# Group A's score operands laid out in runs, its strided queries copied side by side, and negated scores in groups A and B

## The chip, the core and the metric

The kernel runs on one core of a Trainium2 chip. The metric is the device time of one execution in microseconds (us), the median of several runs. TensorE (PE) multiplies, VectorE (DVE), ScalarE (ACT) and GpSimd (POOL) work element by element, and SyncE (SP) issues the DMAs. Each engine takes its own instructions in a fixed order.

## What is computed

One layer of a decoder whose 16 heads fall into four groups of four, all on 2048 tokens of width 1024. Cut to what matters here:

```python
h = rms_norm(x, norm_w) @ w_in            # one projection for all groups
# A: three causal windows, merged by their softmax denominators
DILATED_CONFIGS = ((128, 1), (512, 4), (2048, 16))   # (window, rate r)
for window, rate in DILATED_CONFIGS:
    # tokens folded by residue of r; 128 + 1 keys back within a residue class
    o, lse = banded_attention(fold(q), fold(k), fold(v), table, window // rate, dist_scale=rate)
# B: window of 128 with a learned sink in the softmax
# C: differential attention; D: compressed, selected and window branches
y = concat(A, B, C, D) * silu(gate)
x = x + y @ w_out
```

In each attention a score is q.k plus a bias by distance; the row's maximum is taken off before the exponential.

## The kernel before

**Stages.** The projection runs group by group (C, D, A, B) as a filler behind the attention of C, then D. Its helper `turn` (L735) turns queries and keys to feature rows by PE transposes (L741), and stores them as a high and a low half in the DRAM tensors `TQ` and `TK`, token by token along the row. Then `group_ab` (L1616) computes A and B, with the output projection `out_proj` (L2065) as its filler, and what is left of it ends the program.

**Group A, strided.** `ORDER` lists 32 units: for each head first r=16 and then r=4, four units of four query tiles each. `qk_load` (L1577) brings a head's queries and keys into `QK[h % 2]`: heads 0 and 2 into one big tile, `wb`, for both; heads 1 and 3 into a tile `AQ` for the queries and `keys` for the keys. `a_unit` (L1628) then makes for each query tile two PE matmuls (L1646, the two halves of the keys) of 128 columns, or 256 with the tile before it. Queries (the operand that stays in the array) and keys (the one that streams) are read with a step of r:

```python
def cols(j, i0, n):
    rho, i = divmod(q0 + j, nb)
    c0 = rho + r * 128 * (i - i0)
    return slice(c0, c0 + (n - 1) * r + 1, r)
```

r=16 gives 128 matmuls of 128 columns; r=4 gives 32 of 128 and 96 of 256. One DVE instruction (L1651) adds the bias `H` to the scores out of PSUM, stores the sum and keeps the row's maximum; a second small one (L1656) negates two maxima into column 65 of `AO`; ACT (L1662) takes the exponential with this as bias. Then come transposes (L393), a split into halves (L399 on ACT, L403 on DVE), the products with the values (L422), and the turn back (L435, L439 or L442 and L444). When a head's r=4 units end, `merge` (L1748) joins them with the r=16 result on POOL (L1761 to L1764).

**A with r=1, and B.** After the strided units, 16 units of A with r=1 (`make_a1`, L1829) alternate with 16 of B (`make_b`, L1929). r=1 uses the same `a_unit` with contiguous queries and keys. B has its own scores (L1948), bias and maximum (L1953), maximum with the sink (L1958) and negation (L1959).

**Order.** Nothing is scheduled on the chip. A planner in the kernel, `drive` (L302), writes the order: it keeps a clock per engine, adds an assumed cost for each instruction (`op`), and takes the next ready step of up to three open units, or three matmuls of the output projection where nothing else is ready. POOL also has the gate product of the output projection (L2113) in this stretch.

Of the kernel before, what the change touches and what calls it, by code (L numbers as in the profile page):

```python
# [102 lines left out]
def tile_hybrid_heads(ctx, tc, a):  # L103
# [355 lines left out]
    expo = const.tile([128, 32], F32, name="expo")  # L459
# [8 lines left out]
    sink = const.tile([128, 4], F32, name="sink")  # L468
    nlam = const.tile([128, 1], F32, name="nlam")
# [22 lines left out]
    def raw(t):  # L492
        return t.bitcast(F32)
# [137 lines left out]
    def project(g, first=None):  # L631
# [104 lines left out]
        def turn(t3, j, gi, keep):  # L736
# [3 lines left out]
            for i in range(4):  # L740
                PE.transpose(ps[:, i * 128:(i + 1) * 128], keep[i][0][:, j * 128:(j + 1) * 128], ident)  # L741
# [834 lines left out]

    def qk_load(h, x):  # L1577

        q, k = QK[h % 2]
        n = S // 2  # L1580
        if x < 2:
            aready[h] = load_q(q[:, x * n:(x + 1) * n].unsqueeze(1), "A", h, 1, x * n, n)
        else:
            c = slice((x - 2) // 2 * n, ((x - 2) // 2 + 1) * n)
            aready[h] = mv(raw(k)[x % 2::2, :, c], TK["A"][h * 64:h * 64 + 64, :, c])

# [29 lines left out]
    def group_ab():  # L1616
      with tc.tile_pool(name="aw", bufs=2) as aw, tc.tile_pool(name="as", bufs=1) as as_:
# [8 lines left out]


        def a_unit(r, q0, setup, room, need, source, stats, close):  # L1628
# [5 lines left out]
            def scores(half):  # L1634
                qs, ks, H = source()
                if half == 0:
                    st["P"] = aw.tile([128, 4, 256], F32, name="ap", bufs=3)
                    st["mx"] = aw.tile([128, 4], F32, name="amx", bufs=4)
                P, mx, O = st["P"], st["mx"], stats()
                slot = take("s")  # L1640
                ps = ps_s.tile([128, 512], F32, name="s")
                for j in (2 * half, 2 * half + 1):
                    n = 128 * (1 + prevs[j])
                    s0 = (j % 2) * 256
                    for x in range(2):
                        PE.matmul(ps[:, s0:s0 + n], lhsT=qs(j), rhs=ks(x, j, prevs[j]), start=(x == 0), stop=(x == 1))  # L1646
                        e = op("PE", mm(n) if r == 1 else max(217.0, 0.92 * n)) + 60.0
                for j in (2 * half, 2 * half + 1):
                    n = 128 * (1 + prevs[j])
                    s0 = (j % 2) * 256  # L1650
                    V.tensor_tensor_reduce(P[:, j, :n], ps[:, s0:s0 + n], rev(H, n - 1, n), 1.0, LOW,  # L1651
                                           OP.add, OP.max, mx[:, j:j + 1])
                    e = op("DVE", vv(n), e)
                give(slot, e)
                two = slice(2 * half, 2 * half + 2)
                V.tensor_scalar(O[:, two, 65], mx[:, two], -1.0, None, op0=OP.mult)  # L1656
                e = op("DVE", 72.0, e)

                def weights():
                    for j in (2 * half, 2 * half + 1):  # L1660
                        n = 128 * (1 + prevs[j])
                        A.activation(P[:, j, :n], P[:, j, :n], AF.Exp, bias=O[:, j, 65:66], accum_out=O[:, j, 64:65])  # L1662
                        st["e"] = op("ACT", av(n, 2), e)
                    st["half"] = st.get("half", 0) + 1
                defer(e, weights)

# [22 lines left out]
        def make_a(n):  # L1689
# [8 lines left out]

            def setup():
                if h < 3 and 1 <= n % 8 <= 6:  # L1700
                    qk_load(h + 1, n % 8 - 1)
                if q0 == 0:
# [15 lines left out]
            def source():  # L1718
                Q, K = QK[h % 2]

                def cols(j, i0, n):
                    rho, i = divmod(q0 + j, nb)
                    c0 = rho + r * 128 * (i - i0)
                    return slice(c0, c0 + (n - 1) * r + 1, r)
                return (lambda j: Q[:, cols(j, 0, 128)]), (lambda x, j, p: K[:, x, cols(j, p, 128 * (1 + p))]), Hs[h, r]
# [57 lines left out]
            def room():  # L1783
                if not have_all("A"):
# [3 lines left out]
            u = a_unit(r, q0, setup, room, lambda: max(at("s"), aready[h]), source,  # L1788
                       lambda: tiles(res[h, r][0]), close)
# [39 lines left out]
        def make_a1(m):  # L1829
            q0, h = AORDER[m]  # L1830

            def source():
                Q, K, lo = As[m][0], As[m][1], As[m][7]
                return ((lambda j: Q[:, j * 128:(j + 1) * 128]),
                        (lambda x, j, p: K[:, x, (q0 + j - p - lo) * 128:(q0 + j + 1 - lo) * 128]), raw(A1H(h)))
# [12 lines left out]
            def setup():  # L1848
                if m == 0:
# [3 lines left out]
                    parts += [as_.tile([128, 1024], F32R, name="ow%d" % i) for i in range(2)]  # L1853
# [75 lines left out]
        def make_b(n):  # L1929
# [3 lines left out]
            def scores(i):  # L1933
                Kb, Vb, Qb, lo, _ = Bs[g, t0]
                if i == 0:
                    st["P"] = aw.tile([128, 4, 256], F32, name="ap", bufs=3).rearrange("p (i j) c -> p i j c", i=2)
                    for x in ("mx", "nm", "den"):
                        st[x] = as_.tile([128, 4], F32, name="b" + x, bufs=5)
                P, mx, nm, den = st["P"], st["mx"], st["nm"], st["den"]
# [11 lines left out]
                for j in range(2):  # L1951
                    s0 = j * 256
                    V.tensor_tensor_reduce(P[:, i, j, :n], ps[:, s0:s0 + n], rev(BH[2 * g + j], n - 1, n), 1.0, LOW,  # L1953
                                           OP.add, OP.max, mx[:, i * 2 + j:i * 2 + j + 1])
# [3 lines left out]
                V.tensor_tensor(nm[:, c], mx[:, c], sink[:, 2 * g:2 * g + 2], op=OP.max)  # L1958
                V.tensor_scalar(nm[:, c], nm[:, c], -1.0, None, op0=OP.mult)  # L1959
                e = op("DVE", 260.0, e)  # L1960

                def weights():
                    for j in range(2):
                        x = i * 2 + j
                        A.activation(P[:, i, j, :n], P[:, i, j, :n], AF.Exp, bias=nm[:, x:x + 1],
                                     accum_out=den[:, x:x + 1])
# [271 lines left out]
```

## Time and profile before

| | |
|---|---|
| median of 3 runs | 1769.04 us (1765.94 to 1773.90) |
| profiled execution | 1773.27 us, span 1771.5 us |
| PE busy | 97% of the span |
| DVE, ACT, POOL busy | 76%, 61%, 39% |
| granted TensorE clock, mean | 0.988 |

A line of the profile names the engine, the source line, what is written and read (buffer numbers left out), the shape, and how often. "Busy" of PE is a sum of pipelined matmuls whose durations overlap, so the spacing of matmuls is read from the chain of waits: pieces in order of time, each with its start, its length and the number of instructions in it. The stage of group A's strided units goes from about 1348.5 to 1493.5 us.

### The profile page before, as it was taken

The numbers are of one execution on the slowest core, as the hardware profiler recorded it, in microseconds if no ns is written. First come the engines' busy times: TensorE is split into PE (matmuls) and PEld (weight loads), VectorE is DVE, ScalarE is ACT, GpSimd is POOL, SyncE is SP. The second block draws the span as 40 slices with busy tenths as digits, with TensorE's granted clock in tenths as the row PEclk, the third lists the DMA queues.
The fourth block names the chain that finished last, engine by engine and source line by source line (L and its number), as shares of the span: only waits on it lengthen the run. The fifth ranks groups of instructions, "written<-read, shape, count | busy, mean of one in ns | idle before, by whom it ended". The sixth has DMA issues, their size and how long they took to land.

```text
span 1771.5 us, 31769 instructions
## 1 busy us (share of the span) xinstructions
PE 1709.5 (97%) x10035; PEld 1503.3 (85%) x10035; DVE 1338.3 (76%) x4072; ACT 1072.3 (61%) x2588; POOL 692.8 (39%) x841
## 2 busy tenths in 40 slices
PE   7999999999998999899999999999999999999999
PEld 5878878888887889788888889899979999789987
DVE  4446689898999998488747868888366876888873
ACT  4345466656776756467646656777356776576651
POOL 4567554544544554211255552222521112433331
PEclk9999999999999999899999999999999999999999
DMA  7763554444445424642367533232375778999986
GB/s 246 223 198 108 184 171 144 121 118 139 116 143 159 146 91 152 188 117 88 125 194 226 170 108 96 59 97 85 105 238 169 233 226 259 278 313 311 320 283 213
DMA packets 283480, 308.24 MB, mean 174 GB/s; under 512 B 80256, under 2 KB 201216, under 8 KB 282640
## 3 DMA queue, kind: packets, MB, share of 16 engines
q1 hardware_dynamic: 283312, 306.21, 55.8%
q8 instruction: 80, 1.31, 0.3%
q14 instruction: 88, 0.72, 0.1%
HBM read 219.47 MB, written 86.92 MB: 173 GB/s over the span
## 4 chain that ended last, share of the span: by engine, by line
PE 51%; DVE 3%; issue 1%; DMA 1%; ACT 1%; POOL 0%; SPq 0%; DVEq 0%; POOLq 0%
PE j L840 11%; PE j L2159 9%; PE o L422 9%; PE pt L393 8%; PE s L1646 4%; PE s L950 4%; PE pt L435 3%; PE s L1336 1%; PE pt L2123 1%; PE s L1948 1%; PE s L1435 1%; PE pt L741 0%; DVE pl L403 0%; PE j L1164 0%; DMA xt<-in_xt_dram 0%
## 5 line engine op out<-in xcount | busy, mean ns | idle before, releaser
L840 PE MATMUL j<-wb,xh 128*128 128x512 f32 (+2 forms) x2048 | 618.2, 382 | 18.8 <-DVE wb L622 9.6
L840 PEld LDWEIGHTS j<-wb,xh 128*128 128x128 f32 x2048 | 373.1, 190 | 67.4 <-DVE wb L622 14.5
L840 PE MATMUL j<-wb,xl 128*128 128x512 f32 (+2 forms) x1024 | 385.4, 376 | 0.6 <-POOL xl L577 0.6
L399 ACT ACTIVATE ph<-pt 128x512 fp32r<-128x512 f32 (+4 forms) x486 | 266.0, 575 | 123.5 <-PE pt L393 117.0
L403 DVE TENSOR_TENSOR pl<-pt,ph 128x512 fp32r<-128x512 f32 (+4 forms) x486 | 311.9, 658 | 38.1 <-ACT ph L399 37.2
L840 PEld LDWEIGHTS j<-wb,xl 128*128 128x128 f32 x1024 | 194.3, 190 | 25.7 <-POOL xl L577 1.2
L679 POOL TENSOR_TENSOR ss<-ss,expo 128x6 f32<-128x6 f32 (+2 forms) x64 | 117.4, 1835 | 169.2 <-DVE ss L677 155.3
L577 POOL TENSOR_TENSOR xl<-xt,xh 128x512 fp32r<-128x512 f32 x112 | 149.2, 1333 | 9.3
L371 ACT ACTIVATE ot<-o 128x512 f32<-128x512 f32 (+1 forms) x160 | 81.5, 509 | 106.4 <-PE o L422 105.9
L571 POOL TENSOR_SCALAR xh<-xt 128x512 fp32r<-128x512 f32 x128 | 84.6, 661 | 134.2 <-DMA xt<-in_xt_dram 65.5
L950 PE MATMUL s<-keys,Q 128*128 128x512 f32 (+3 forms) x320 | 113.6, 400 | 12.7 <-DVE mx L952 6.1
L2113 POOL TENSOR_TENSOR xt<-xt,sq 128x512 f32<-128x512 f32 x32 | 41.3, 1290 | 184.2 <-PE s L1646 66.2
L952 DVE CUSTOM_DVE_ANT_0 prow<-s,Hs 128x512 f32<-128x512 f32 (+3 forms) x160 | 95.1, 604 | 19.3 <-PE s L950 18.8
L1066 DVE SCALAR_TENSOR_TENSOR pa<-pb,ra,pa 128x1024 f32<-128x1024 f32 (+4 forms) x96 | 107.5, 1147 | 2.3
L660 ACT ACTIVATE stqk<-j 128x512 f32<-128x512 f32 x64 | 38.2, 597 | 113.5 <-PE j L840 111.0
L952 DVE CUSTOM_DVE_ANT_0 pa<-s,H 128x512 f32<-128x512 f32 (+3 forms) x160 | 93.8, 603 | 14.0 <-PE s L950 11.3
L952 DVE CUSTOM_DVE_ANT_0 pb<-s,H 128x512 f32<-128x512 f32 (+3 forms) x160 | 93.1, 603 | 7.2 <-PE s L950 6.5
L1662 ACT ACTIVATE ap<-ap,AO 128x128 f32<-128x128 f32 (+1 forms) x192 | 86.4, 456 | 17.7 <-DVE AO L1656 17.5
L1050 ACT ACTIVATE pa<-pa,nm 128x128 f32<-128x128 f32 (+7 forms) x64 | 76.9, 1202 | 31.5 <-DVE nm L958 31.0
L674 DVE TENSOR_REDUCE ss<-sq 128x6 f32<-128x384 f32 (+2 forms) x64 | 39.3, 614 | 69.9 <-ACT sq L664 69.9
L435 PE MATMUL pt<-ident,ot 128*128 128x128 f32 x512 | 85.0, 278 | 3.1 <-ACT ot L371 2.6
L1050 ACT ACTIVATE pb<-pb,nm 128x128 f32<-128x128 f32 (+7 forms) x64 | 76.8, 1200 | 16.5 <-DVE nm L958 16.3
(267 smaller groups left out, 4207.4 us busy)
## 6 DMA issues: line engine op xcount, KB each, us to landing
xt<-in_xt_dram SPq DMA_DIRECT2D x128, 256.0 KB, 3.3
xr<-in_x_dram SPq DMA_DIRECT2D x16, 512.0 KB, 5.4
Q<-tqC SPq DMA_DIRECT2D x64, 128.0 KB, 3.4
DQ<-tqD SPq DMA_DIRECT2D x16, 512.0 KB, 4.8
raw<-gate_d SPq DMA_DIRECT2D x32, 256.0 KB, 4.2
stqk<-in_x_dram SPq DMA_DIRECT2D x32, 256.0 KB, 4.8
acc_d<-stqk SPq DMA_DIRECT2D x32, 256.0 KB, 4.5
stqk<-acc_d SPq DMA_DIRECT2D x32, 256.0 KB, 4.5
```

The costliest lines, as they stand in the source:

```text
L393: PE.transpose(ps[:rows, x * 128:(x + 1) * 128], src(), ident)
L399: A.activation(ph[:rows, :n], ps[:rows, :n], AF.Copy)
L403: V.tensor_tensor(pl[:rows, :n], ps[:rows, :n], ph[:rows, :n], op=OP.subtract)
L422: PE.matmul(u["po"][:, c0:c0 + wd], lhsT=lhsT(), rhs=x[:rows, col:col + wd], start=u["k"] == 1, stop=u["k"] == total, skip_group_check=True)
L435: PE.transpose(ps[:, i * 128:(i + 1) * 128], ot[:, i * 128:(i + 1) * 128], ident)
L577: G.tensor_tensor(l, xt, h, op=OP.subtract)
L679: G.tensor_tensor(ss[:, :nh], ss[:, :nh], expo[:, :nh], op=OP.pow)
L840: PE.matmul(ps[:, :n], lhsT=xx[:, ks], rhs=W[k][ww][:, lo:hi], start=(k == 0 and i == 0), stop=(k == KT - 1 and i == 2))
L950: PE.matmul(ps[:, :n], lhsT=q(), rhs=k[:, k0:k0 + n], start=(i == 0), stop=(i == np_ - 1))
L952: V.tensor_tensor_reduce(st["row"][:, k0:k0 + n], ps[:, :n], rev(H, t * 128 + 127 - k0, n), 1.0, LOW, OP.add, OP.max, st["mx"][:, ci:ci + 1])
L1050: A.activation(row[:, :nk], row[:, :nk], AF.Exp, bias=nm, accum_out=den[:, i, m:m + 1])
L2159: PE.matmul(ps, lhsT=xx[:, ks], rhs=OW[half, (k, c)][ww], start=(x == 0 and k == 0 and i == 0), stop=(x == len(halves) - 1 and k == 3 and ...
```

## The change

Keys of A are stored in another order of columns: the transposes of `turn` write each tile of 128 tokens by residue of 16, so that 8 keys of one residue stand side by side. Scores then stream the keys in runs of 8: r=16 takes one run of each tile; r=4 takes four residues, tile by tile; r=1 takes 16 residues. For r=4 and r=1 the scores stand in PSUM in another order of keys than the bias, so the DVE instruction reads PSUM with a jump at each element. The queries of a strided unit are copied side by side by POOL (`gather_more`), into four half tiles of the two `ow` tiles that take output weights later. The r=16, r=4 and r=1 query gains, and B's, are multiplied by -0.125 in place of 0.125, and the bias vectors of A's and B's heads are negated; so the DVE instruction takes a minimum, which is at once the negated maximum, ACT gets a scale of -1, and L1656 and L1959 go.

```diff
-        V.tensor_scalar(gains[:, 1:4], gains[:, 1:4], 0.125, None, op0=OP.mult)
+
+        V.tensor_scalar(gains[:, 1:3], gains[:, 1:3], -0.125, None, op0=OP.mult)
+        V.tensor_scalar(gains[:, 3:4], gains[:, 3:4], 0.125, None, op0=OP.mult)
...
+        V.tensor_scalar(nsink, sink, -1.0, None, op0=OP.mult)
...
-        V.memset(tp[96:128, :], NEG)
+        V.memset(tp[96:128, 0:8], -NEG)
+        V.memset(tp[96:128, 8:16], NEG)
+        V.tensor_scalar(tb[0:96, 0:8], tb[0:96, 0:8], -1.0, None, op0=OP.mult)
...
-                PE.transpose(ps[:, i * 128:(i + 1) * 128], keep[i][0][:, j * 128:(j + 1) * 128], ident)
+                to = ps[:, i * 128:(i + 1) * 128]
+                if g == "A" and j >= 2:
+                    to = to.rearrange("p (r i) -> p i r", r=16)
+                PE.transpose(to, keep[i][0][:, j * 128:(j + 1) * 128], ident)
...
+        def gather_more():
+            while len(AC) < len(ORDER) and ORDER[len(AC)][0] in aloaded and free("AC", 4) < INF:
+                n = len(AC)
+                h, r, q0 = ORDER[n]
+                hd = alloc("AC", 4)
+                C = OW4[hd[1] % 4 // 2][:, hd[1] % 2 * 512:hd[1] % 2 * 512 + 512]
+                Q = QK[h % 2][0].rearrange("p (c r) -> p r c", r=r)
+                if r == 16:
+                    G.tensor_copy(C.rearrange("p (j c) -> p j c", j=4), Q[:, q0:q0 + 4])
+                else:
+                    G.tensor_copy(C, Q[:, q0 // 4])
+                AC[n] = (C, hd, op("POOL", 1150.0, max(aready[h], hd[2])))
...
-                        e = op("PE", mm(n) if r == 1 else max(217.0, 0.92 * n)) + 60.0
+                        e = op("PE", mm(n)) + 60.0
...
-                    V.tensor_tensor_reduce(P[:, j, :n], ps[:, s0:s0 + n], rev(H, n - 1, n), 1.0, LOW,
-                                           OP.add, OP.max, mx[:, j:j + 1])
+
+                    fr = ps[:, s0:s0 + n] if r == 16 else ps[:, s0:s0 + n].rearrange("p (b u) -> p u b", b=16 // r)
+                    V.tensor_tensor_reduce(P[:, j, :n], fr, rev(H, n - 1, n), 1.0, -LOW,
+                                           OP.add, OP.min, O[:, j, 65:66])
...
-                two = slice(2 * half, 2 * half + 2)
-                V.tensor_scalar(O[:, two, 65], mx[:, two], -1.0, None, op0=OP.mult)
-                e = op("DVE", 72.0, e)
...
-                return (lambda j: Q[:, cols(j, 0, 128)]), (lambda x, j, p: K[:, x, cols(j, p, 128 * (1 + p))]), Hs[h, r]
+                K, C = QK[h % 2][1], AC[n][0]
+                if r == 16:
+                    K = K.rearrange("p x (t r c) -> p x r t c", t=16, r=16)
+                    ks = lambda x, j, p: K[:, x, q0 + j]
+                else:
+                    K = K.rearrange("p x (t s a c) -> p x a s t c", s=4, a=4, c=8)[:, :, q0 // 4]
+                    ks = lambda x, j, p: K[:, x, :, (j - p) * 4:(j + 1) * 4]
+                return (lambda j: C[:, j * 128:(j + 1) * 128]), ks, Hs[h, r]
...
-                        (lambda x, j, p: K[:, x, (q0 + j - p - lo) * 128:(q0 + j + 1 - lo) * 128]), raw(A1H(h)))
+                        (lambda x, j, p: K[:, x].rearrange("p (t b c) -> p b t c", b=16, c=8)[:, :, q0 + j - p - lo:q0 + j + 1 - lo]),
+                        raw(A1H(h)))
...
-                V.tensor_tensor(nm[:, c], mx[:, c], sink[:, 2 * g:2 * g + 2], op=OP.max)
-                V.tensor_scalar(nm[:, c], nm[:, c], -1.0, None, op0=OP.mult)
-                e = op("DVE", 260.0, e)
+                V.tensor_tensor(nm[:, c], nm[:, c], nsink[:, 2 * g:2 * g + 2], op=OP.min)
+                e = op("DVE", 130.0, e)
```

The planner's assumed cost of a strided score falls with it (`mm(n)`), so the order of the whole stage is another one. A copy is written into the order when its head's last load has been issued and one of the four half tiles is free, and the scores of a unit wait for its copy.

On PE, the order at the start of the strided stage, before (`s` are scores, `j` the output projection, `pt` transposes, `wb` here the queries and keys of head 0):

```order
L1646 MATMUL s<-wb 128x128 x12
L2159 MATMUL j<-wb,xh 128x512 x2
L2159 MATMUL j<-wb,xl 128x512
L1646 MATMUL s<-wb 128x128 x4
L2123 MATMUL pt<-ident,xt 128x128 x4
L393 MATMUL pt<-ident,ap 128x128 x4
```

and now (`ow` are the copied queries, L1675 the scores, L2199 the output projection):

```order
L1675 MATMUL s<-wb,ow_17192 128x128 x8
L2199 MATMUL j<-wb,xh 128x512 x2
L2199 MATMUL j<-wb,xl 128x512
L1675 MATMUL s<-wb,ow_17192 128x128 x8
L2199 MATMUL j<-wb,xh 128x512 x2
L2199 MATMUL j<-wb,xl 128x512
L393 MATMUL pt<-ident,ap 128x128 x4
L1675 MATMUL s<-wb,ow_17193 128x128 x8
```

Three matmuls of the output projection now stand behind each unit of eight scores, where before one such three stood behind twelve scores. Over the strided stage their number goes from 90 to 144, and behind the last score from 237 to 180.

On POOL, the order from group D's last sum (L1553) over the first two merges (L1761 to L1764) before, with what each instruction waits for:

```order
L1553 TENSOR_TENSOR Os<-Os,yps 128x128 [waits DMAHW1_49,Pool_49]
L2113 TENSOR_TENSOR xt<-xt,sq 128x512 [waits DMAHW4_49,DMAHW5_49,DVE_49,PE_49] x2
L1761 TENSOR_TENSOR AO<-AO,mg 128x16x65 [waits DMAHW2_49,PE_49,DMAHW7_49,Activation_49,Pool_49]
L1761 TENSOR_TENSOR AO<-AO,mg 128x16x65 [waits DMAHW7_49,DMAHW2_49,DVE_49]
L1763 TENSOR_TENSOR AO<-AO 128x16x65 [waits Pool_49]
L1764 COPY AO<-mgn 128x16
L2113 TENSOR_TENSOR xt<-xt,sq 128x512 [waits DMAHW0_49,DMAHW1_49,DVE_49,PE_49]
```

and now, around the first merge (L1801 to L1804; L1651 and L1653 are the copies for r=16 and r=4, from `AQ` those of head 1, from `wb` those of head 2; L2153 is the gate product):

```order
L1653 COPY ow_17192<-AQ 128x512 [waits PE_49,Pool_49] x2
L2153 TENSOR_TENSOR xt<-xt,sq 128x512 [waits DMAHW4_49,DMAHW3_49,DVE_49]
L1653 COPY ow_17193<-AQ 128x512 [waits PE_49,Pool_49] x2
L1801 TENSOR_TENSOR AO<-AO,mg 128x16x65 [waits Activation_49]
L1801 TENSOR_TENSOR AO<-AO,mg 128x16x65 [waits DMAHW6_49,DMAHW1_49,DVE_49]
L1803 TENSOR_TENSOR AO<-AO 128x16x65 [waits Pool_49]
L1804 COPY AO<-mgn 128x16
L1651 COPY ow_17192<-wb 128x512 [waits DMAHW4_49,DMAHW3_49,DMAHW5_49,DMAHW1_49,DMAHW6_49,DMAHW0_49,PE_49]
L1651 COPY ow_17192<-wb 128x512 [waits PE_49]
```

The first copy of head 2 stands behind the merge of head 0 and waits for six DMA queues, those of its queries and of its keys. The merge of head 1 stands in the same way ahead of head 3's copies; all 32 copies are ahead of the merge of head 2.

## Rows read from the trace of the kernel before

**Rows 1.** The page, first part: engine, busy us, share of the span, instructions.

```profile
PE 1709.5 (97%) x10035; PEld 1503.3 (85%) x10035; DVE 1338.3 (76%) x4072; ACT 1072.3 (61%) x2588; POOL 692.8 (39%) x841
```

**Rows 2.** Busy us (and instructions) by stretch: PE, PEld, DVE, ACT, POOL; clock, DMA share, GB/s.

```profile
1348.50:1493.50 145.00, 144.32 (x896) 137.38 (x895) 105.95 (x421) 99.88 (x346) 25.16 (x18) 1.00 0.77 239
1493.50:1720.00 226.50, 221.60 (x1463) 198.02 (x1462) 194.88 (x667) 154.11 (x467) 76.15 (x102) 0.99 0.95 296
1720.00:1771.00 51.00, 47.63 (x221) 38.37 (x219) 20.09 (x30) 7.30 (x13) 9.06 (x7) 0.99 0.70 226
```

**Rows 3.** The chain of waits from 1350 to 1493 us, shares by line.

```profile
by line: PE s L1646 39.1%; PE o L422 16.8%; PE j L2159 14.6%; PE pt L393 11.9%; PE pt L435 9.4%; DVE AO L1656 2.4%; DVE ap L1651 1.9%; DVE pl L403 1.4%; PE pt L2123 1.3%; issue 0.5%; DVE xl L2133 0.4%; DVE sq L2110 0.4%; DVE AO L444 0.2%; D
```

**Rows 4.** The chain of waits, single pieces: start, us, engine and line, instructions.

```profile
1400.87 0.84 PE o L422 x8
...
1403.98 1.99 PE s L1646 x8
...
1416.00 1.72 PE s L1646 x8
...
1549.13 0.93 PE s L1646 x8
...
1730.17 5.54 PE j L2159 x24
```

**Rows 5.** Groups by form, PE, 1345 to 1495 us, line L1646.

```profile
L1646 PE MATMUL s<-wb 128*128 128x128 f32 x82 | 21.2, 396 | 0.0
...
L1646 PE MATMUL s<-keys,AQ 128*128 128x128 f32 x80 | 21.0, 395 | 0.0
...
L1646 PE MATMUL s<-wb 128*128 128x256 f32 x54 | 16.8, 438 | 0.0
...
L1646 PE MATMUL s<-keys,AQ 128*128 128x256 f32 x48 | 15.8, 454 | 0.0
```

**Rows 6.** Line L1646: duration in ns, min, median and max.

```profile
L1646 PEld LDWEIGHTS s<-keys,AQ x128: 291/310/337, 1377.3 to 1490.2; 128*128 128x128 f32 x128
```

**Rows 7.** Groups by form, POOL, whole span.

```profile
L571 POOL TENSOR_SCALAR xh<-xt 128x512 fp32r<-128x512 f32 x128 | 84.6, 661 | 134.2 <-DMA xt<-in_xt_dram 65.5 <-PE j L840 30.9 <-PE j L1164 17.6
...
L2113 POOL TENSOR_TENSOR xt<-xt,sq 128x512 f32<-128x512 f32 x32 | 41.3, 1290 | 184.2 <-PE s L1646 66.2 <-DVE sq L2110 61.8 <-DMA tkB<-th 15.5
```

**Rows 8.** POOL in order of time, and the merge's waits in its queue (line L1761).

```profile
1349.60 0.46 POOL L1553 TENSOR_TENSOR Os<-Os,yps 128x128 f32<-128x128 f32 x1
...
1395.40 3.82 POOL L1761 TENSOR_TENSOR AO<-AO,mg 128x1040 f32<-128x1040 f32 x2 [4.25 <-ACT mg L1758]
...
1399.30 2.42 POOL L1763 TENSOR_TENSOR AO<-AO 128x1040 f32<-128x1040 f32 x1
...
L1761 POOLq EVENT_SEMAPHORE  x6: 17/43/21916, 1389.9 to 1515.6; - x6
```

**Rows 9.** PE in order of time, first scores of head 0 and of head 2.

```profile
1350.43 1.77 PE L1646 MATMUL s<-wb 128*128 128x128 f32 x8
...
1409.65 1.96 PE L1646 MATMUL s<-wb 128*128 128x128 f32 x8
```

**Rows 10.** DMA: head 2's last key load, and issues with KB and us to landing.

```profile
1402.15 0.76 SPq L156 DMA_DIRECT2D wb<-tkA  x1
...
wb<-tkA SPq DMA_DIRECT2D x8, 512.0 KB, 7.4
```

**Rows 11.** Groups by form, DVE, 1348 to 1495 us, and a piece of the chain.

```profile
L403 DVE TENSOR_TENSOR pl<-pt,ph 128x512 fp32r<-128x512 f32 x30 | 20.5, 682 | 1.0 <-ACT ph L399 0.9
...
L1651 DVE CUSTOM_DVE_ANT_0 ap<-s,AH 128x256 f32<-128x256 f32 x48 | 18.9, 418 | 3.5 <-PE s L1646 3.5
...
L1656 DVE TENSOR_SCALAR AO<-amx 128x2 f32<-128x2 f32 x65 | 17.8, 273 | 2.4
...
L439 DVE TENSOR_REDUCE AO<-pt 128x256 f32<-128x512 f32 x19 | 13.1, 688 | 11.4 <-PE pt L435 11.4
...
1395.91 1.44 DVE AO L1656
```

More of the change, by code (lines that the diff above doesn't have):

```diff
@@ L458, in tile_hybrid_heads @@
     nw = const.tile([128, KT], F32, name="nw")
-    expo = const.tile([128, 32], F32, name="expo")
+    expo = const.tile([128, 16], F32, name="expo")
     V.memset(expo, -0.5)
@@ L468, in tile_hybrid_heads @@
     sink = const.tile([128, 4], F32, name="sink")
+    nsink = const.tile([128, 4], F32, name="nsink")
     nlam = const.tile([128, 1], F32, name="nlam")
@@ L1585, in qk_load @@
             aready[h] = mv(raw(k)[x % 2::2, :, c], TK["A"][h * 64:h * 64 + 64, :, c])
+        if x == 5:
+            aloaded.add(h)
     ORDER = [(h, r, q0) for h in range(4) for r in (16, 4) for q0 in range(0, 16, 4)]
@@ L1624, in h_load, with a_unit @@
             Hs[h, r] = H
-        def a_unit(r, q0, setup, room, need, source, stats, close):
+        OW4 = [as_.tile([128, 1024], F32R, name="ow%d" % i) for i in range(2)]
+        AC = {}
+        def gather_more():
[10 more added lines that the diff above has]
+                AC[n] = (C, hd, op("POOL", 1150.0, max(aready[h], hd[2])))
+        def a_unit(r, q0, setup, room, need, source, stats, close, scored=lambda: None):
             nb = 16 // r
@@ L1637, in scores @@
                     st["P"] = aw.tile([128, 4, 256], F32, name="ap", bufs=3)
-                    st["mx"] = aw.tile([128, 4], F32, name="amx", bufs=4)
-                P, mx, O = st["P"], st["mx"], stats()
+                P, O = st["P"], stats()
                 slot = take("s")
@@ L1661, in weights @@
                         n = 128 * (1 + prevs[j])
-                        A.activation(P[:, j, :n], P[:, j, :n], AF.Exp, bias=O[:, j, 65:66], accum_out=O[:, j, 64:65])
+                        A.activation(P[:, j, :n], P[:, j, :n], AF.Exp, bias=O[:, j, 65:66], scale=-1.0,
+                                     accum_out=O[:, j, 64:65])
                         st["e"] = op("ACT", av(n, 2), e)
@@ L1665, in scores @@
                 defer(e, weights)
+                if half:
+                    scored()
             jobs = []
@@ L1697, in tiles, with scored @@
                 return O[:, q0:q0 + 4] if nb == 1 else O[:, q0 // nb::r]
+            def scored():
+                release(AC[n][1], T["PE"] + 60.0)
+                defer(T["PE"] + 100.0, gather_more)
             def setup():
+                if n == 0:
+                    gather_more()
                 if h < 3 and 1 <= n % 8 <= 6:
                     qk_load(h + 1, n % 8 - 1)
+                    if n % 8 == 6:
+                        defer(aready[h + 1], gather_more)
                 if q0 == 0:
@@ L1786, in room @@
                 return 0.0 if q0 else free("AO", 4)
-            u = a_unit(r, q0, setup, room, lambda: max(at("s"), aready[h]), source,
-                       lambda: tiles(res[h, r][0]), close)
+            u = a_unit(r, q0, setup, room, lambda: max(at("s"), aready[h], AC[n][2] if n in AC else INF), source,
+                       lambda: tiles(res[h, r][0]), close, scored)
             u["after"] = after
@@ L1852, in setup @@
                     parts += [QK[1][0][:, i * 1024:(i + 1) * 1024] for i in range(2)]
-                    parts += [as_.tile([128, 1024], F32R, name="ow%d" % i) for i in range(2)]
+                    parts += OW4
                     out_weights("AB", [(w[:, 0:512], w[:, 512:1024]) for w in parts])
@@ L1936, in scores @@
                     st["P"] = aw.tile([128, 4, 256], F32, name="ap", bufs=3).rearrange("p (i j) c -> p i j c", i=2)
-                    for x in ("mx", "nm", "den"):
+                    for x in ("nm", "den"):
                         st[x] = as_.tile([128, 4], F32, name="b" + x, bufs=5)
-                P, mx, nm, den = st["P"], st["mx"], st["nm"], st["den"]
+                P, nm, den = st["P"], st["nm"], st["den"]
                 t = t0 + i
@@ L1952, in scores @@
                     s0 = j * 256
-                    V.tensor_tensor_reduce(P[:, i, j, :n], ps[:, s0:s0 + n], rev(BH[2 * g + j], n - 1, n), 1.0, LOW,
-                                           OP.add, OP.max, mx[:, i * 2 + j:i * 2 + j + 1])
+                    V.tensor_tensor_reduce(P[:, i, j, :n], ps[:, s0:s0 + n], rev(BH[2 * g + j], n - 1, n), 1.0, -LOW,
+                                           OP.add, OP.min, nm[:, i * 2 + j:i * 2 + j + 1])
                     e = op("DVE", vv(n), e)
@@ L1965, in weights @@
                         A.activation(P[:, i, j, :n], P[:, i, j, :n], AF.Exp, bias=nm[:, x:x + 1],
-                                     accum_out=den[:, x:x + 1])
+                                     scale=-1.0, accum_out=den[:, x:x + 1])
                         st[i] = op("ACT", av(n, 2), e)
```

6 lines of the change are left out of this document (1 added, 5 removed).

## The prediction

> **What bounds the kernel now.** I read the page's busy shares first, then the busy time by stretch, then the chain of waits inside the stretches, and last single groups by form.
>
> TensorE (PE) is busy 97% of the span [rows 1]. The change works almost wholly in group A's two strided parts, from 1348.5 to 1493.5 us. There PE is busy 144.3 of 145.0 us, VectorE (DVE) 106.0, ScalarE 99.9, GpSimd (POOL) 25.2, and the granted clock is full [rows 2]. In the stretch behind it (r=1 scores of A, group B and the output projection) PE is busy 221.6 of 226.5 us, and at the end, with the output projection alone, 47.6 of 51.0 [rows 2]. Busy PE need not be PE at its peak, so the chain decides: between 1350 and 1493 it runs over PE for 39.1% on the score line L1646 alone, and most of the rest lies on the products, transposes and output projection of the same engine [rows 3]. The reader should see that PE issues without a gap there. Output-projection matmuls fill the holes between attention units, and what is not filled in is done at the end at 5.54/24 = 0.231 us each [rows 4]. So a microsecond taken from PE's scores comes off the end, wherever the order puts the fillers.
>
> **PE, the scores.** L1646 has 162 matmuls of 128 columns and 102 of 256 in the stretch [rows 5]; 2 and 6 of these are the first r=1 unit, so 160 and 96 are strided. Eight strided ones of 128 take 1.72 us, 0.215 each; eight of 256 take 1.99 us, 0.249 each [rows 4]. Loading one strided query block takes 310 ns at the median [rows 6], longer than the matmul spacing. Contiguous ones of the same size: eight value products of 128 take 0.84 us, 0.105 each, and eight r=1 scores of 256 take 0.93 us, 0.116 each [rows 4]. With queries side by side and keys in runs of 8 this saves 160 x 0.110 = 17.6 and 96 x 0.133 = 12.8, together 30.4 us.
>
> This takes a run of 8 keys to be read as fast as a contiguous row, which no row shows. The nearest rows are contiguous (0.116) and a jump at every key (0.249). At the far end the 96 gain nothing (12.8 us lost), and the 120 two-tile r=1 scores, whose keys become alternating runs, lose 16.0: 28.8 us together. If each jump costs its share, one in 8, it is 0.0166 x 216 = 3.6 us. I take 0, since 7 of 8 steps are those of the contiguous row. The Trainium skill (SBUF — State Buffer, section "Door 1: The DMA port swizzle") says SBUF is read in lines of 16 bytes, and that only an access that moves to a new line each time pays. By that the r=4 step of 16 bytes pays, which the 0.249 agrees with, and a run of 32 bytes does not: the sum stays.
>
> **PE, the key transposes.** 32 transposes of A's keys (two blocks of heads, four groups of four tiles) now write PSUM at every eighth column. No row shows that. Below, it costs nothing; above, I use what jumps at every element cost this engine in reading, 0.133 per 256 columns on 0.116, so some 0.12 x 32 = 3.9 us. I take 3.9, as the jump is at every column. The Trainium skill (PSUM — Partial Sum Buffer, section "Specifications (TRN2)") says that any non-contiguous access slows matmuls significantly; it gives no figure, and no row here shows the case. By that rule 0 is out and the sum would lie at 3.9 us or over it; by the row alone it lies between 0 and 3.9.
>
> **POOL, the copies.** 32 copies of 128x512. A one-input pass of this size takes 0.66 us on POOL, a two-input one 1.29 [rows 7]; strided reading should lie between or a little above, so 21 to 41 us are added to an engine with 120 us free in this stretch. That is cover, if the copies come in time. Each is issued up to four units ahead (some 16 us at 4 us a unit). At two places there is no such lead. At the start POOL ends group D's last sum at 1350.06 and PE begins the scores at 1350.43 [rows 8, 9]: one copy between them costs 1 us. At head 2 the last key load goes out at 1402.15 and takes 7.4 us to land, so it lands about when the scores begin at 1409.65 [rows 9, 10]; the copy now stands between load and score and waits for the keys too (they lie in the same tile), so 1.3 us. For heads 1 and 3 the queries have a tile of their own, loaded early: nothing. Behind a score that waits stands all of PE's fixed order. Sum 2.3 us, with bounds 0 and 5.
>
> **DVE.** Out go 96 + 32 small negations. In the stretch 65 of them take 17.8 us, 0.273 each [rows 11], since some stretch, one to 1.44 us while POOL merges [rows 8, 11]. The one of 1.44 lies on the chain, where the line has 2.4% of 143 us, 3.4 us [rows 3, 11]. What is late next is the subtraction queued behind it on DVE, so I take 1.0 us gained, of 0 to 3.4. The 156 two-tile reductions of r=4 and r=1 now read PSUM with jumps. The reduction over halves, which reads 512 with jumps, takes 0.688 us against 0.682 for a straight pass [rows 11], so I take nothing. At twice their 0.418 [rows 11] the r=4 ones add 40 us, which DVE's 39 free us and the 17.8 of negations just hold. The extra sink and table operations at the start are four short DVE instructions there, covered by the projections. ScalarE only gets a scale of -1 in the same instructions, and no DMA is added.
>
> **Sum.** -30.4 + 3.9 + 2.3 - 1.0 = -25.2 us. The profiled execution took 1773.27 us, so 1748.1; it lies 4.2 us above the median of the runs shown, 1769.04, so I forecast 1744. Its own range goes from 1735 (transposes and waits cost nothing, the DVE gain is whole: -33.8) to 1751 (a share for each jump, 3.9, waits of 5, no DVE gain: -17.9).
>
> **Rivals.**
> *Copies held in POOL's queue.* The merge of a head stands in the queue ahead of the next-but-one head's copies (heads 2 and 3). Once in this stage the queue stood 21.9 us at a merge, which then runs 6.3 us [rows 8]. If that falls on a merge with copies behind it, they come 28.2 us later against a lead of 16 us, so PE waits some 13 us: 1757. At both heads it is 1770. Against it: at the first merge the wait was 4.25 us [rows 8], and the long one belongs to a merge that has no copies behind it now. It decides from a wait of about 10 us on.
> *Fillers not fed.* Counted over the two orders, 144 output-projection matmuls stand in the stage in place of 90. The DMA engines, 77% busy there [rows 2], would carry the loads of 54/24, some two row blocks, more in 17 us less (30.4 - 12.5). If the 54 x 0.231 = 12.5 us can't be fed, PE waits that long: 1756. Against it: at 95% DMA share PE stays 98% busy in the next stretch [rows 2].
> *The change does not do what it says: runs cost what strides cost.* Then 28.8 us are given back: 1773, no change. For it: only a step at every key has been timed.
> *Slower: a jump costs more than the strided step.* Each start of a run in PE's key reads stalls it. This decides from 0.273 us per 256-column score on; at 0.34 the 216 scores add 216 x 0.224 = 48 us: 1792. Against it: strided reading has a jump at every key and takes 0.249.
>
> **How the numbers follow.** About 0.5% (8.8 us) is what a measurement of this kernel can tell from no change, so faster is below 1760.2 and slower above 1777.9. Chances: the forecast 0.70; copies held 0.13, of which 0.03 for both heads; fillers not fed 0.05; runs as strides 0.08; slower 0.04. Faster is 0.70 + 0.10 + 0.05 = 0.85, same 0.03 + 0.08 = 0.11, slower 0.04. The range reaches over the forecast and over the two rivals near 1757, with 5 us of their own bound, and leaves out 1770 and above: 1735 to 1762.
>
> **What would show it.** In the profile after: scores of the strided part at 0.105 to 0.116 us in the chain, weight loads near 190 ns, r=1 scores still 0.93 us for eight, POOL copies of 0.7 to 1.3 us, no PE wait of over 2 us on POOL, the stage some 16 us shorter and the end part some 12. Wrong it is if the two-tile scores stay above 0.2 us, if PE waits for copies at heads 2 and 3, or if DVE passes of 256 rise well above 0.42 us.

## The result and the profile after

The changed kernel takes 1816.36 us (median of 4 runs, 1809.77 to 1819.69) against 1770.37 for the kernel before on the same chip (4 runs): a ratio of 1.0264, 95% interval 1.0243 to 1.0285. It is slower by 46 us, where 25 us faster was forecast. The profiled execution took 1815.60 us, its span is 1813.8. The page's first part and the slices of the span, of the kernel after, answer to [rows 1]:

```profile
span 1813.8 us, 31733 instructions
...
PE 1701.3 (94%) x10035; PEld 1489.7 (82%) x10035; DVE 1316.4 (73%) x3948; ACT 1068.1 (59%) x2576; POOL 725.0 (40%) x873
...
PE   7999999999989999899999999999999998687888
...
PEclk9999999999999999999999999999999999888889
```

From the second slice on PE is over 80% busy, mostly over 90%, until the last seven of the 40; there its busy share falls, and the granted clock with it in five of them. The busy time by stretch, of the kernel after (columns as in [rows 2]), with the strided parts, the r=1 part with group B, and the end:

```profile
1344.80:1473.00 128.20, 127.87 (x931) 117.64 (x931) 92.58 (x355) 95.64 (x335) 60.01 (x49) 0.97 0.88 280
1473.00:1760.00 287.00, 233.25 (x1398) 207.47 (x1397) 178.69 (x582) 149.63 (x452) 70.35 (x95) 0.88 0.74 228
1760.00:1814.00 54.00, 48.90 (x238) 39.19 (x237) 24.58 (x51) 12.32 (x28) 11.47 (x12) 0.99 0.62 200
```

The strided stage became shorter, as was forecast, and PE has no gap in it. The stretches here and in [rows 2] do not end at the same event, though: 1493.5 lies behind the first r=1 unit of the kernel before, 1473 ahead of that of the kernel after. Between the same events, from the first strided score to the first r=1 score, it is 130.9 us (1344.80 to 1475.73) instead of 140.6 (1350.43 to 1491.07). From there to the end of the last score it is 284.3 us instead of 213.0, and behind that 53.8 instead of 67.5. In the second stretch above PE stands idle for 53.8 us (287.00 less 233.25), and was granted 0.88 of its clock.

What the strided stage shows, first the chain of waits of the kernel after (start, us, what; eight scores of an r=16 unit, then eight of r=4, which are two of 128 and six of 256), then its groups by form:

```profile
1416.05 0.85 PE s L1675 x8
...
1421.17 1.03 PE s L1675 x8
```

```profile
L1675 PEld LDWEIGHTS s<-keys,ow 128*128 128x128 f32 x128 | 17.0, 191 | 1.5 <-PE pt L393 0.5 <-issue 0.4
L1653 POOL CAST ow<-AQ 128x512 fp32r<-128x512 f32 x8 | 8.9, 1122 | 12.3 <-PE s L1675 12.3
L1682 DVE CUSTOM_DVE_ANT_0 ap<-s,AH 128x256 f32<-128x256 f32 x46 | 17.9, 420 | 0.8 <-PE s L1675 0.7
L1675 PE MATMUL s<-wb,ow 128*128 128x128 f32 x80 | 13.3, 304 | 1.9 <-POOL ow L1651 1.9
L750 PE MATMUL pt<-ident,stqk 128*128 128x128 f32 x240 | 35.8, 280 | 2.0 <-POOL stqk L689 1.2 <-DVE pl L403 0.7
```

Eight scores take 0.85 and 1.03 us instead of 1.72 and 1.99 [rows 4]. A weight load takes 191 ns on average instead of a median of 310 [rows 6], a POOL copy 1.12 us, a DVE pass of 256 with jumps 420 ns against 418 [rows 11]. The 240 q/k transposes, the 32 with strided PSUM writes among them, take 35.8 us, 280 ns each; the same group of the kernel before:

```profile
L741 PE MATMUL pt<-ident,stqk 128*128 128x128 f32 x240 | 35.7, 280 | 2.2 <-POOL stqk L683 1.4 <-DVE pl L403 0.7
```

So the loss lies in the r=1 part. Two views of the kernel after say by what; the longest waits of PE from 1475 us on (engine, line, what it waited for: us in total, times, longest), and the chain of 1473 to 1760 by line, with the first of its pieces that name the load:

```profile
PE s L1675 <- DMA wb<-tkA: 37.4, 8, 8.0
PE s L1675 <- issue: 11.1, 2, 7.6
PE pt L2163 <- POOL xt L2153: 1.9, 2, 1.6
```

```profile
by line: PE j L2199 26.1%; DMA wb<-tkA 19.0%; PE s L1675 7.5%; PE pt L393 6.4%; PE o L422 6.0%; PE s L1989 5.9%; PE pt L435 4.2%; SPq L156 3.7%; issue 3.4%; DVE stqk L2205 2.3%; DMA stqk<-in_x_dram 2.1%; PE pt L2163 1.8%; DMA out_dram<-stqk
...
1542.48 5.30 DMA wb<-tkA
...
1565.48 6.18 DMA wb<-tkA
...
1584.00 4.97 DMA wb<-tkA
```

Nothing of this kind stood in the stretch of the kernel before: its costliest line of waits there is 3.1 us (shown with e3_before_view below). Loads of r=1 keys are 19% of the chain of 287 us, 55 us. Which load it is shows only in the timeline of one unit of the kernel after (start, us, engine, line, out<-in; in brackets idle time before and its releaser):

```profile
1541.13 0.74 PE L1675 MATMUL s<-wb 128*128 128x256 f32 x4
1541.28 0.32 SPq L156 DMA_DIRECT2D wb<-tqA  x1
1541.89 1.18 SPq L156 DMA_DIRECT2D wb<-tkA  x2
...
1547.92 1.19 PE L1675 MATMUL s<-wb 128*128 128x256 f32 x4 [5.13 <-DMA wb<-tkA]
```

PE does the first half of a unit's scores at 1541.13. Then SP issues the loads of the **next** unit, into the other slot of the same tile wb. The second half of the same unit's scores, whose keys had landed before the first half ran, waits for these loads to land. The wait also costs time after it has ended. Two stretches of the change show the granted clock of PE, the first behind a wait for POOL's first copy, which comes up again below, the second behind this one (columns as in [rows 2]):

```profile
1346.00:1350.00 4.00, 4.00 (x16) 3.61 (x16) 2.39 (x16) 2.61 (x12) 4.00 (x5) 0.50 0.94 297
...
1547.90:1549.15 1.25, 1.23 (x5) 1.25 (x6) 0.00 (x1) 0.00 (x0) 0.00 (x0) 0.50 0.13 32
```

At 1541 the granted clock was 1.00; after 5.1 idle us PE works at 0.50, the lower of its two levels, and four scores take 1.19 us instead of 0.74. The list of the two programs' instructions with the semaphores that they wait for says the same without times. Of each program in its written order, on PE the scores of the last unit but one, in halves, and on SP the first of the last unit's two key loads:

```
before  L1646 MATMUL s<-wb 128x256 [waits DMAHW3_49,DMAHW2_49,DMAHW1_49]
        L156 DMA wb<-tkA 64x2x640 [waits DMAHW3_49]
        L1646 MATMUL s<-wb 128x256 x4
after   L1675 MATMUL s<-wb 128x256 [waits DMAHW6_49,DMAHW5_49,DMAHW4_49]
        L156 DMA wb<-tkA 64x2x640 [waits DMAHW1_49,PE_49]
        L1675 MATMUL s<-wb 128x256 [waits DMAHW2_49,DMAHW1_49]
```

Before, a unit waits once, for its own three loads. After, the second half waits for two DMA queues more, and a load waits for PE.

### The profile page after: what moved, and what is told of

Its sections match the earlier page's. It is cut to its first block, busy times and chain, and to the rows that moved or that the text cites. A ratio compares the mean times of both kernels' runs of the same rounds, so it can differ in the third digit from the quotient of the medians.

```text
span 1813.8 us, 31733 instructions
## 1 busy us (share of the span) xinstructions
PE 1701.3 (94%) x10035; PEld 1489.7 (82%) x10035; DVE 1316.4 (73%) x3948; ACT 1068.1 (59%) x2576; POOL 725.0 (40%) x873
## 4 chain that ended last, share of the span: by engine, by line
PE 46%; DMA 4%; DVE 3%; issue 1%; ACT 1%; POOL 1%; SPq 1%; POOLq 0%; DVEq 0%; ACTq 0%
PE j L849 11%; PE o L422 8%; PE j L2199 7%; PE pt L393 7%; PE s L959 4%; DMA wb<-tkA 3%; PE s L1675 3%; PE pt L435 2%; PE s L1345 1%; PE s L1989 1%; SPq L156 1%; DMA stqk<-in_x_dram 1%; PE pt L2163 1%; PE s L1444 1%; DVE stqk L2205 1%
## 5 line engine op out<-in xcount | busy, mean ns | idle before, releaser
L961 DVE CUSTOM_DVE_ANT_0 pa<-s,H 128x512 f32<-128x512 f32 (+3 forms) x160 | 93.9, 604 | 13.7 <-PE s L959 11.1
L2153 POOL TENSOR_TENSOR xt<-xt,sq 128x512 f32<-128x512 f32 x32 | 41.1, 1284 | 141.0 <-DVE sq L2150 84.8
L2199 PE MATMUL j<-wb,xh 128*128 128x512 f32 x256 | 87.0, 422 | 0.0
```

The source lines that it names most:

```text
L961: V.tensor_tensor_reduce(st["row"][:, k0:k0 + n], ps[:, :n], rev(H, t * 128 + 127 - k0, n), 1.0, LOW, OP.add, OP.max, st["mx"][:, ci:ci + 1])
L2199: PE.matmul(ps, lhsT=xx[:, ks], rhs=OW[half, (k, c)][ww], start=(x == 0 and k == 0 and i == 0), stop=(x == len(halves) - 1 and k == 3 and ...
```

## The experiments

**Theory 1**: the rearranged view of the r=1 keys (residue, tile, runs of 8) hides from the dependency tracking that a read of one slot of wb and a load into the other are disjoint, so a wait that no data needs was written into the program. **Rival 2**: the loads land late by themselves. **Rival 3**: runs of 8, or jumps in PSUM, are slow in the r=1 scores.

**e2_own.** A tile of its own, two buffers, for these keys; group B's keys and queries take the freed columns of wb:

```diff
-            K = wb[:, base + 512:base + 1792].rearrange("p (i c) -> p i c", i=2)
+            K = as_.tile([128, 2, 640], F32R, name="A1K", bufs=2)
...
-            Kb = as_.tile([128, 2, 384], F32R, name="BK", bufs=2)
+            base = 8192 + hd[1] % 2 * 2432 + 512
+            Kb = wb[:, base:base + 768].rearrange("p (i c) -> p i c", i=2)
...
-            Qb = as_.tile([128, 2, 256], F32R, name="BQ", bufs=2)
+            Qb = wb[:, base + 768:base + 1280].rearrange("p (i c) -> p i c", i=2)
```

> The changed kernel with the r=1 keys in a tile of their own, A1K, with two buffers; group B's keys and queries take the freed columns of wb. Every engine keeps the order of its instructions. Theory 1 (the second half of a unit's r=1 scores waits for the next unit's key load, because both lie in one tile and the rearranged view of the keys hides that they are disjoint): the 12 waits of 4 to 8 us on the key load are gone, the stretch behind the strided one is back at some 226 us, the median is 1745 us (1737 to 1753), 70 us below the change. Rival 2 (the key loads land late by themselves, SP or the DMA engines being crowded): 1805 to 1820, since the same loads stand at the same places. Rival 3 (runs of 8 in the r=1 scores, or jumps in DVE's reading of them, are slow): 1805 to 1820, since both are unchanged.

Measured: 1749.90 us, ratio to before 0.9885 (0.9869 to 0.9901), 66 us below the change. (The kernel before took 1768.1 to 1770.4 us beside the runs of this document, so times of two runs compare to about 2 us.) The same place in the timeline of e2_own, and its stretches:

```profile
1540.54 0.38 SPq L156 DMA_DIRECT2D wb<-tqA  x1
1541.21 1.20 SPq L156 DMA_DIRECT2D A1K<-tkA  x2
...
1542.09 0.73 PE L1675 MATMUL s<-A1K,wb 128*128 128x256 f32 x4
...
1543.59 0.65 PE L1675 MATMUL s<-A1K,wb 128*128 128x256 f32 x4
```

```profile
1345.00:1473.00 128.00, 126.10 (x929) 115.87 (x928) 92.05 (x351) 94.77 (x332) 61.21 (x50) 0.99 0.89 281
1473.00:1700.00 227.00, 217.07 (x1434) 192.08 (x1433) 183.89 (x599) 154.21 (x467) 71.82 (x97) 0.99 0.93 295
1700.00:1750.00 50.00, 44.23 (x210) 35.27 (x208) 20.46 (x37) 8.09 (x16) 9.86 (x11) 0.99 0.59 193
```

The same load goes out before the same second half, which now runs 0.8 us after the first half ends. In 227 us PE does 1434 matmuls, 36 more than the change did in 287. Rivals 2 and 3 fall: loads, views, runs and jumps are all still there. The clock is back at 0.99, so its fall to 0.88 came with the idle gaps and was not a cause beside them. Of the 60 us that the stretch loses, 44 are PE's idle time (53.8 to 9.9); the other 16 are work that was slower at the lower clock (four r=1 scores after a wait took 1.19 us against 0.65 here).

**e5_plain_view.** The change with the plain view for r=1:

```diff
-                        (lambda x, j, p: K[:, x].rearrange("p (t b c) -> p b t c", b=16, c=8)[:, :, q0 + j - p - lo:q0 + j + 1 - lo]),
+                        (lambda x, j, p: K[:, x, (q0 + j - p - lo) * 128:(q0 + j + 1 - lo) * 128]),
```

> The changed kernel, but the r=1 scores read their keys in the order in which they lie in wb, as the kernel before does (the scores then meet the biases of other keys). Theory 1: no wait on the next load, 1745 us (1737 to 1753), the same as with the tile of its own. Rival 2 (loads late by themselves): 1805 to 1820. Rival 3 (runs of 8 are read slowly): faster than the version with its own tile by what the runs cost, 3.6 us at a share for each jump, 16 us at the price of strides; eight two-tile scores in 0.93 us here against more there.

Measured: 1749.91 us, ratio 0.9884 (0.9864 to 0.9904), the same as e2_own to 0.01 us. Taking the view away does as much as taking the shared tile away. And runs of 8 cost the r=1 scores next to nothing. The same eight scores in the chain of e2_own (runs) and of e5_plain_view (contiguous):

```profile
1518.21 0.96 PE s L1675 x8
```

```profile
1518.45 0.93 PE s L1675 x8
```

That is 0.004 us for each two-tile score, some 0.5 us for the 120, of the 16.0 that the prediction held possible. Those of r=4 take more, (1.03 - 2 x 0.106) / 6 = 0.136 us for 256 in the change's chain; why they differ is not shown.

**e3_before_view.** The other direction: the kernel before, with the rearranged view alone.

```diff
-                        (lambda x, j, p: K[:, x, (q0 + j - p - lo) * 128:(q0 + j + 1 - lo) * 128]), raw(A1H(h)))
+                        (lambda x, j, p: K[:, x].rearrange("p (t b c) -> p b t c", b=16, c=8)[:, :, q0 + j - p - lo:q0 + j + 1 - lo]),
+                        raw(A1H(h)))
```

> The kernel before with one edit: the r=1 scores read their keys through the rearranged view (16 residues, tiles, runs of 8; the scores then meet the biases of other keys). Theory 1: 12 or so new waits of 4 to 6 us on the next unit's key load, so some 50 to 65 us more: 1820 to 1835. Rival 2 (loads late because of the change's new order and speed): 1770, no change. Rival 3 (slow runs): at most 16 us more, 1774 to 1786, with no new wait on a load.

Measured: 1833.12 us, ratio 1.0354 (1.0337 to 1.0371), 63 us more. The waits of PE behind the strided stage, of e3_before_view:

```profile
PE s L1646 <- DMA wb<-tkA: 41.2, 8, 8.9
PE s L1646 <- issue: 5.6, 1, 5.6
PE o L422 <- DVE pl L403: 3.1, 2, 1.8
```

The third line stands in the kernel before with the same figures; the first two are the view's. So the view is enough to bring the wait, without copied queries, another key order, negative scores or a faster strided stage. Which property of the view defeats the tracking (its three dimensions, or steps that do not fall from left to right) was not tried.

**e7_keys and e6_queries.** Which half of the 30.4 us the queries give, and which the keys. e7_keys is e2_own with strided query loads (the copies are made and not read); e6_queries is the change with the keys in natural order, the plain r=1 view, and copied queries.

```diff
 e7_keys
...
-                return (lambda j: C[:, j * 128:(j + 1) * 128]), ks, Hs[h, r]
+                def qs(j):
+                    rho, i = divmod(q0 + j, nb)
+                    c0 = rho + r * 128 * i
+                    return Q[:, c0:c0 + 127 * r + 1:r]
+                return qs, ks, Hs[h, r]
...
 e6_queries
-                if g == "A" and j >= 2:
-                    to = to.rearrange("p (r i) -> p i r", r=16)
...
+                ks = lambda x, j, p: K[:, x, cols(j, p, 128 * (1 + p))]
...
```

> The version with r=1 keys in a tile of their own, but the strided scores load their queries from the strided rows as before; GpSimd's copies are still made and not read. It tells which half of the 30.4 us the queries give. If strided query loads were the limit (310 ns each at the median before), the strided scores fall back to 0.215 and 0.249 us and the time to 1775; if the strided keys were the limit, 0.105 and 0.128 us stay and the time is 1745. Theory 1 says nothing on it. My guess lies between: 128 columns back at 0.2 us, 256 columns between, 1765.

> The changed kernel without its new order of the keys: A's keys lie in natural order, the strided scores read them with steps of 16 and 4 elements as before, the r=1 view is the plain one; the queries are copied side by side by GpSimd and the negative scores stay. PE keeps the order of the change. Theory 1 expects no wait on the next r=1 load, since the view is the plain one. What the strided scores cost now: the run with strided queries and keys in runs of 8 showed 1.71 us for eight scores of 128 and 1.94 for eight of 256, nearly the kernel before's 1.72 and 1.99, so the query's weight load set their pace. Theory A (the queries were the whole limit, the keys' step costs nothing): 0.85 and 1.02 us for eight, 1750 us or up to 4 less. Theory B (the step of 4 elements, 16 bytes, is slow for the keys too, hidden behind the weight load before): the 96 scores of 256 stay near 0.24 us, 11 us more, 1761; if the step of 16 elements is slow too, up to 1771.

Measured: e7_keys 1770.69 us, ratio 1.0010 (0.9998 to 1.0023), 20.8 above e2_own; e6_queries 1760.37 us, ratio 0.9952 (0.9935 to 0.9969), 10.5 above. Chains of e7_keys, then of e6_queries, each with eight of an r=16 unit and eight of r=4, beside 0.85 and 1.03 of the change (of e6_queries also the second half of an r=4 unit, four of 256):

```profile
1425.72 1.70 PE s L1675 x8
...
1441.93 1.94 PE s L1675 x8
```

```profile
1391.98 0.93 PE s L1673 x4
...
1424.21 0.88 PE s L1673 x8
...
1432.90 1.67 PE s L1673 x8
```

With strided queries the keys' order gains next to nothing (1.70 and 1.94 against 1.72 and 1.99 [rows 4]): the query's weight load sets the pace. With queries side by side the keys' step of 16 costs almost nothing (0.88), and the step of 4 costs what remains: four of 256 take 0.93 us, 0.233 each. The guess of 1765 for e7_keys was too low, since I gave the keys a share there that they do not have. For e6_queries theory B's 1761 was met.

**e8_negative and e10_neg_order.** The kernel before with negative scores alone. In e8 the planner no longer counts the removed negations, as in the change; in e10 their times stay in its sums, so every engine but DVE keeps the written order of before:

```diff
 e10_neg_order against e8_negative
+                e = op("DVE", 72.0, e)
...
-                e = op("DVE", 130.0, e)
+                e = op("DVE", 260.0, e)
```

> The kernel before with the negative scores alone (queries and keys strided as before, no copies). It takes away 128 small negations on DVE and moves nothing else on purpose, though the written order of the work shifts. The prediction's term: 1.0 us gained (0 to 3.4), 1769; a rival: the shifted order costs or gains as much as 5 us either way, 1765 to 1775.

> The kernel before with the negative scores, and with the times of the removed negations (72 and 130 ns) left in the planner: every engine but DVE then keeps the written order of the kernel before, and DVE only loses the negations. Theory O (the 8.7 us that the negative scores cost alone come from the shifted written order: SP stood 7.1 us before a load of merged outputs, with group B's keys queued behind): 1767 us, the 1.0 us of the prediction gained, 1765 to 1769. Rival I (the changed instructions themselves cost it): 1777, as with the negative scores in their own order.

Measured: e8 1776.81 us, ratio 1.0056 (1.0035 to 1.0078); e10 1763.54 us, ratio 0.9976 (0.9965 to 0.9987). The negations gain 4 us (0.24% of 1769; 2 to 6 by the interval) where the order is kept, and the order that the planner writes without them loses 13 us (1776.81 less 1763.54). Waits of SP, then of PE, of e8_negative from 1470 us on:

```profile
SPq L156 <- POOL AO L1800: 7.1, 1, 7.1
```

```profile
PE s L1986 <- DMA BK<-tkB: 4.1, 1, 4.1
PE s L1673 <- DVE bnm L1991: 3.8, 1, 3.8
```

SP's queue stands 7.1 us at a transfer that needs POOL's merge, the loads of group B's keys are queued behind it, and PE waits for them, then for DVE. These two waits are 7.9 of the 13 us; the rest is not traced. Rival I falls.

**e11_own_order and e9_plain_sign.** e11 is e2_own with the negations' times left in the planner (the edit of e10); e9 is the same order with positive scores and the small negations.

> The changed kernel with r=1 keys in a tile of their own, and with the times of the removed negations left in the planner. Nothing but the written order differs from the version with its own tile (1749.9 us). Theory O: the order is worth some us either way; without the waits on the load of group B's keys (2.8 us) and on the gate's product (2.4 us) that the other order showed in the stretch behind the strided one, 1745; 1741 to 1755. Rival I: 1750, no change.

> The same kernel in the same written order, but with positive scores and the small negations of the kernel before on DVE: query copies, key order and the tile of its own are all that is left of the change. Theory O: 1.0 us above the version with negative scores in this order (0 to 3.4), some 1746. Rival I: 8.7 us below it, 1741.

Measured: e11 1766.17 us, ratio 0.9986 (0.9973 to 0.9999); e9 1773.79 us, ratio 1.0036 (1.0023 to 1.0049). Both expectations missed. The written order is worth 16 us between e2_own and e11, with the sign reversed against e8 and e10: here the planner's leaner sums write the better order. PE's longest waits in e11_own_order behind the strided stage:

```profile
PE pt L2165 <- POOL xt L2155: 6.7, 3, 3.1
PE pt L393 <- DVE gst L444: 5.2, 1, 5.2
```

e2_own has 2.4 us of the first and none of the second. All waits of PE behind the stage add up to 17.6 us against 10.8, which is 7 of the 16 us; where the rest goes is not shown. In this order the negations cost 7.6 us (e9 less e11).

## Why the prediction was wrong

The direction, the number and the range were wrong, by one step: that the r=1 part changes only in how fast PE reads its keys. The prediction costed "the 120 two-tile r=1 scores, whose keys become alternating runs" as a read rate, at 0 of 0 to 16.0 us, and that 0 was right (some 0.5 by e2_own and e5). What the new view does to the waits was not asked; the sentence that no DMA is added was true, and a wait on a DMA was added all the same. Measured, the term is +63 us on the kernel before (e3) and 66 us in the change (change less e2_own). Neither the four rivals nor the list of signs held it: the slower rival was put on jumps in the read, which e5 shows to cost the r=1 scores next to nothing. The written order of PE was compared row by row, but without the waits of each row, where it stood to be read.

The other steps, against e2_own, which is the change without that wait:

- **PE scores, -30.4.** Right in the main. By the chain's pieces the saving is 160 x (0.215 - 0.106) + 96 x (0.26 - 0.136) = 29.3 us. One reading was loose: "eight of 256" in [rows 4] are two of 128 and six of 256, so a strided 256 took (1.99 - 2 x 0.215) / 6 = 0.26 us and not 0.249; the sum hardly moves. Part of it shows in the strided stage and part behind the last score, where fewer fillers are left (stretches below). Undone one at a time, queries are 20.8 us and keys 10.5 (e7, e6).
- **Key transposes, +3.9.** The lower end held: 35.8 us for the 240 against 35.7, so 0.
- **POOL copies, +2.3.** Right in place, short in size: one wait of 1.9 us at the first copy, none at heads 2 and 3; 1.07 to 1.12 us a copy. Behind this wait PE was granted 0.50 of its clock for some us (1346 to 1350 in the change, shown above; 1350 to 1352 in e2_own), which the term did not count. By the clock in stretches of 2 us that is, as an estimate, 1.7 us of work in e2_own and 3.4 in the change, so 3.6 and 5.3 us with the wait. The rival of copies held in POOL's queue did not occur.
- **DVE, -1.0.** Too small: 4 us (2 to 6) in e10, over its bound of 3.4 at the median, and 7.6 beside the copies (e9 less e11). That DVE's PSUM jumps are free was right (420 against 418 ns). The count of 156 two-tile reductions was not: there are 48 of r=4 [rows 11] and 60 of r=1, so the far end would have been 20 us and not 40. The sum did not use it.
- **Written order.** Not in the sum. Moving two planner costs of 72 and 130 ns moved the time by 13 us one way (e8, e10) and 16 the other (e2_own, e11).

e2_own lies 20 us below before and not 25. Stretches between the same events show where: from the first strided score to the first r=1 score, on to the end of the last score, and on to the end (columns as in [rows 2]), of the kernel before and then of e2_own:

```profile
1350.43:1491.07 140.64, 139.96 (x869) 133.54 (x869) 102.44 (x411) 97.44 (x339) 24.30 (x16) 1.00 0.77 239
1491.07:1704.05 212.98, 208.08 (x1387) 186.46 (x1387) 185.09 (x637) 147.83 (x448) 69.33 (x91) 0.99 0.96 300
1704.05:1771.50 67.45, 63.58 (x315) 52.18 (x313) 32.27 (x69) 16.00 (x40) 15.88 (x18) 0.99 0.69 223
```

```profile
1347.92:1476.58 128.66, 128.66 (x953) 118.74 (x953) 94.49 (x361) 98.34 (x345) 60.13 (x49) 0.99 0.90 285
1476.58:1695.32 218.74, 208.81 (x1377) 184.73 (x1376) 176.95 (x576) 146.41 (x444) 70.21 (x95) 0.99 0.94 296
1695.32:1749.10 53.78, 48.91 (x239) 39.23 (x237) 24.58 (x51) 12.31 (x28) 11.47 (x12) 1.00 0.62 201
```

The strided stage is 12.0 us shorter with 84 matmuls more in it, and the end 13.7 us shorter, as forecast for the fillers. The part between, which the prediction left as it was, is 5.8 us longer with as much work: PE idles 9.9 us there instead of 4.9, the longest new waits being 2.8 us on loads of group B's keys. Why they are new is not shown. (The two profiled executions lie 22.4 us apart; the last 2.5 are ahead of the stage.)

With the wait on the key loads gone the version beats both kernels: 1749.90 us, within the range of 1735 to 1762 that was given for the change. In part that is luck, as errors cancel: the transposes were priced too high and the gain of the negations too low, while the copies and the r=1 part cost more than the sum had.

## What to carry to other kernels

Where an access is rewritten as another view of a tile that holds two buffers, compare the waits of the two programs and not only their order: a wait on a load that was issued after the data had landed is a false one, and a tile for each buffer removes it. A step costed by its read rate can be free in that and still add a wait. Where a planner writes the order, give a small edit a control with the old planner costs before its gain is believed.

## What the runs showed of the hardware

In these scores a strided operand costs by what is slower, its weight load or its moving columns. A strided weight load keeps eight scores of 128 at 1.70 to 1.72 us for either order of the keys. Moving columns at a step of 4 elements take 0.233 / 256 = 0.91 ns each, where a contiguous 256 takes 0.116 us [rows 4], 0.45 ns each. At a step of 16 they take 0.88 / 8 / 128 = 0.86 ns at most; a contiguous 128 takes nearly as much, 0.105 us [rows 4] or 0.82 ns each, so the price of this step is not seen. Runs of 8 take 0.004 us more than contiguous rows for 256 in the r=1 scores, and 0.020 more in those of r=4.

The Trainium skill (SBUF — State Buffer, section "Door 1: The DMA port swizzle") says that every access which moves to a new line of 16 bytes pays. The step of 16 bytes (0.91 ns a column against 0.45) and the runs of 32 bytes, which cost little, agree; for the step of 64 bytes no run here shows it.

Strided PSUM writes of the transposes cost nothing that shows (the 240, of which 32 are strided, take 280 ns each on average in both kernels), nor did jumps in DVE's reading (420 ns against 418). The Trainium skill (PSUM — Partial Sum Buffer, section "Specifications (TRN2)") says that any non-contiguous access slows matmuls significantly; these traces do not show that, and the measurement decides here.

Behind two idle stretches PE worked at the lower of its two clock levels: it was granted 0.50 from 1547.90 us on, behind 5.1 idle us, and 0.50 from 1346 to 1350 us, behind the 1.9 us at the first copy. In e7_keys, where PE does not wait for the copies, it stays at 1.00 from 1336 to 1370 us.

DVE's small negations are slower beside POOL: 273 ns each on average before [rows 11], 393 in e9_plain_sign, where POOL also copies (group of VectorE in the strided stage):

```profile
L1683 DVE TENSOR_SCALAR AO<-amx 128x2 f32<-128x2 f32 x60 | 23.6, 393 | 2.7 <-DVE amx L1678 0.5
```

Where no POOL instruction runs beside it, a negation takes 168 to 171 ns in both kernels. That is 56 of 65 before and 32 of 60 in e9_plain_sign; the others overlap a merge, a gate product or a copy, and nearly all take longer, up to 1.9 us.
